# Attention: the queries' rotary product on VectorE instead of GpSimd

## The chip, the cores and the metric

The kernel runs on one core of a Trainium2 chip. That core has a matrix engine (TensorE, PE in the profile; PEld is its weight load), three engines for elementwise work (VectorE = DVE, ScalarE = ACT, GpSimd = POOL), a queue engine that issues most transfers (SyncE = SP), and 16 DMA engines. The engines run their own instruction queues in order and wait for each other through semaphores. The metric is the device time of one execution in microseconds.

## The reference

The program is two layers of a diffusion backbone for 512 latent tokens and 256 context tokens, width 1024, in float32. Layer 0 mixes tokens by windowed grouped-query attention (16 query heads of 64, 4 key heads), layer 1 by a chunked retention. Each layer ends in a gated feed-forward block. Only the latent stream is returned. The change lies in layer 0, in the step between the query projection and the scores:

```python
q_x, k_x, v_x = jnp.split(h_x @ w_qkv, [qd, qd + kvd], axis=-1)
q_x = rope_2d(rms_norm(q_x.reshape(B, S, N_HEADS, HEAD_DIM), q_gain), tables)

def rotate_axis(x, cos, sin):
    x1, x2 = jnp.split(x, 2, axis=-1)
    return jnp.concatenate([x1 * cos - x2 * sin, x1 * sin + x2 * cos], axis=-1)
```

So each query element is multiplied by a cosine, its partner 16 places away by a sine, and the two products are added. Context queries (`s == 1` in the kernel) have no positions and skip the step. After it come scores over a window of 128 and all context keys, a softmax with a sink logit, the value product and the output projection.

## The kernel before

Activations lie transposed, with channels on the 128 partitions and tokens along the free dimension. A query tile `j` (0 to 7) holds two heads: 128 channels by 512 latent and 256 context tokens. Every large product is made of three reduced-precision matmuls (`mm3`, lines 148 to 150): weight and activation are each split into a high and a low part. The splits of weights (`next_w`, lines 140 and 141) and of other operands (`split`, lines 165 and 166) cost one ScalarE copy and one VectorE subtraction each.

`make_q(j)` returns four pieces: projections of the latent and context tokens, with `shape(s)` behind each, and `norms()`. `shape(0)` is what changes. ScalarE takes the projection out of PSUM into `qn` (564) and its squares into `sq` (565). VectorE writes the partner channels into `sw` by a shuffle (569). GpSimd multiplies `qn` by the cosines (570) while VectorE multiplies `sw` by the sines (571), and VectorE adds the two (572). ScalarE and VectorE then split the result into high and low parts per head (578 to 581). `norms()` computes the inverse root mean squares by a small matmul (590) and short instructions (593, 597); they enter the softmax as scales. The keys' step, `rope_key`, has the same four elementwise instructions all on VectorE.

An attention block is one key head with its four query heads and 128 queries, 24 blocks in all: four head groups, each with four latent and two context blocks. For each head, `score` copies the bound for the row maximum (668, GpSimd), multiplies queries by keys (684, TensorE), and adds the mask and takes the row minimum (685, VectorE). For each pair of heads there follow a small product (691, VectorE), two exponentials with row sums (101, ScalarE), a reciprocal (695, VectorE) and two normalisations in SBUF (698, GpSimd). `turn` transposes the probabilities by the identity (707, TensorE) and copies them out of PSUM (709, ScalarE and VectorE alternately). `output` multiplies by the values (719) and copies the result (734, VectorE). After the first three groups `split_o` splits their results for the output projection (165, 166).

The program gives the order of the pieces: the tiles 0 and 1 first, then two further tiles within each of the first three head groups, after their second and fourth blocks. In that part only the first tile's TensorE work is in an order written out by hand. Everywhere else a planner takes each engine's instructions, gives each a cost of its own and orders the queue by it, so blocks, projections and splits are interleaved. The order is fixed when the kernel is built. A projection's matmuls thus lie between the scores, transposes and value products of other blocks, and the first output-projection tiles (lines 148 to 150 on the `h` tiles) between those of the last group. SP's queue brings the weights (line 122), then the residual streams (174, 179).

Of the kernel before, what the change touches and what calls it, by code (L numbers as in the profile page):

```python
# [49 lines left out]
def dit_kernel(ctx, tc, xT, cT, crow, small, consts, masks, tabs0, tabs1, jtab, adaQ, adaN, adaT, wst, out):  # L50
    nc = tc.nc
    mult, add, sub = ALU.mult, ALU.add, ALU.subtract
# [9 lines left out]
    def T(pool, cols, tag, bufs, dt=F32):  # L62
        return pool.tile([P, cols], dt, tag=tag, bufs=bufs, name=tag)

    def pj(n=512):
        return T(psJ, 512, "pj", 2)[:, :n]
# [69 lines left out]
    def next_w(pool, own=2, raw=None):  # L136

        raw = raw or w_raw()
        hi, lo = w_parts(pool, own)
        nc.scalar.copy(hi, raw)  # L140
        nc.vector.tensor_tensor(lo, raw, hi, op=sub)  # L141
        return hi, lo

    def mm3(o, w, x, first, last):

        whi, wlo = w
        xhi, xlo = x
        nc.tensor.matmul(o, whi, xhi, start=first, stop=False)  # L148
        nc.tensor.matmul(o, wlo, xhi, start=False, stop=False)  # L149
        return nc.tensor.matmul(o, whi, xlo, start=False, stop=last)  # L150
# [32 lines left out]
    def t_sq(n):  # L183
        return T(rp, 512, "sq", 2)[:, :n]

    def t_hn(n):
        return T(rp, 512, "hn", 2)[:, :n]

    def t_y(s):
        return T(rp, NTOK[s], f"y{s}", 1)  # L190

    def neg_half_rstd(y, z, tot, count):

        lnexp(y, tot, AF.Ln, scale=1.0 / count, bias=eps)
        lnexp(y, y, AF.Exp, scale=-0.5)
        nc.scalar.activation(z, y, AF.Square, scale=0.5 / math.sqrt(count))
        nc.vector.scalar_tensor_tensor(z, tot, count * EPS, z, add, mult)
        nc.vector.scalar_tensor_tensor(y, z, -0.75, y, add, mult)
# [194 lines left out]
    rope0 = T(akv, 1024, "rope0", 1)  # L393
# [153 lines left out]
    def make_q(j, raw=None):  # L547

        w = next_w(ap, 1, raw)
        qs = T(ap, 64, "qs", 4)[:, 0:36].rearrange("p (f n) -> p f n", f=3)
        sqs, o = [], [None, None]

        def part(s, k0, k1):
            if k0 == 0:
                o[s] = pj(NTOK[s])
            for k in range(k0, k1):
                mm3(o[s], (w[0][:, k * P:(k + 1) * P], w[1][:, k * P:(k + 1) * P]), h[s][k], k == 0, k == KT - 1)

        def shape(s):
            n = NTOK[s]
            sq, qn = t_sq(n), t_hn(n)
            nc.scalar.activation(qn, o[s], AF.Identity, scale=qk_gain[:, 0:1])
            nc.scalar.activation(sq, o[s], AF.Square)
            sqs.append(sq)
            if s == 0:
                sw = t_y(s)
                nc.vector.stream_shuffle(sw, qn, swap16)
                nc.gpsimd.tensor_tensor(qn, qn, rope0[:, 0:512], op=mult)  # L570
                nc.vector.tensor_tensor(sw, sw, rope0[:, 512:1024], op=mult)
                nc.vector.tensor_tensor(qn, qn, sw, op=add)
            qa = T(ap, 512, "q", 9, F32R)
            if s == 0:
                qb = T(ap, 512, "q", 9, F32R)
            else:
                qa, qb = qa[:, 0:SC], qa[:, SC:2 * SC]
            nc.scalar.copy(qa[0:64, :], qn[0:64, :])
            nc.scalar.copy(qb[64:128, :], qn[64:128, :])
            nc.vector.tensor_tensor(qa[64:128, :], qn[0:64, :], qa[0:64, :], op=sub)  # L580
            nc.vector.tensor_tensor(qb[0:64, :], qn[64:128, :], qb[64:128, :], op=sub)
            q[2 * j, s] = qa
            q[2 * j + 1, s] = qb

        def norms():
            tot = pj(12)
            for s, sq in enumerate(sqs):
                for b in range(NTOK[s] // P):
                    c = 8 * s + 2 * b
                    nc.tensor.matmul(tot[:, c:c + 2], sq[:, b * P:(b + 1) * P], bd[:, 0:P:64], start=True, stop=True)  # L590
            y, u, z = qs[:, 0], qs[:, 1], qs[:, 2]
            neg_half_rstd(y, z, tot, HD)
            nc.vector.scalar_tensor_tensor(u, tot, HD * EPS, y, add, mult)
            ue = u.rearrange("p (b e) -> p e b", e=2)
            for e in range(2):
                hd = 2 * j + e
                nc.vector.tensor_scalar(ue[:, e], ue[:, e], nsink[:, hd:hd + 1], -4.0 / HD, op0=mult, op1=mult)
                stats[hd] = qs

        def first():  # L600
            part(0, 0, 5)

        def second():
            part(0, 5, KT)
            shape(0)
            part(1, 0, 3)

        def third():
            part(1, 3, KT)
            shape(1)  # L610

        return [first, second, third, norms]
# [1178 lines left out]
```

## Time and profile before

| | |
|---|---|
| runs (3) | 1774.48 to 1779.74 us, median 1777.0 us |
| profiled execution | 1777.24 us, span 1775.5 us |
| TensorE busy | 1717.1 us (97%) |
| VectorE busy | 1356.0 us (76%) |
| ScalarE busy | 841.2 us (47%) |
| GpSimd busy | 134.4 us (8%) |
| mean granted TensorE clock | 0.994 |
| line 570 on GpSimd | 8 instructions, 12.9 us, first start 88.9 us, last 254.4 us |

Times in the traces are microseconds from the start of the span. Attention runs from about 88 us to 328 us; before it lie the modulation and the key and value projections, after it the output projection, the feed-forward block and layer 1. Matmuls are pipelined, so their recorded durations overlap: the spacing of their starts says what one costs. A number in square brackets behind an instruction is the time its engine stood idle just before it, with the instruction that ended the wait. A wait for several instructions is put down to the one that came last.

### The profile page before, as it was taken

How to read it: one execution, taken by the hardware profiler on the slowest of the kernel's cores; microseconds unless marked ns; L12 is line 12 of the kernel's file. 1: busy time of each engine (PE TensorE's matmuls, PEld its weight loads, DVE VectorE, ACT ScalarE, POOL GpSimd, SP SyncE). 2: the span in 40 equal slices, each digit the busy share in tenths (PEclk: the TensorE clock that was granted, in tenths of full speed). 3: DMA queues.
4: the chain of work that ended last, by engine and by line, in shares of the span. 5: the costliest groups of instructions: out<-in, count | busy, mean ns of one | idle time of the engine just before them, and what ended most of it. 6: DMA issues, size and time to landing. Idle time of an engine off the chain costs nothing.

```text
span 1775.5 us, 27602 instructions
## 1 busy us (share of the span) xinstructions
PE 1717.1 (97%) x10852; PEld 1527.1 (86%) x10852; DVE 1356.0 (76%) x2365; ACT 841.2 (47%) x1477; POOL 134.4 (8%) x275
## 2 busy tenths in 40 slices
PE   6899999999999999999998999999999999999999
PEld 4777776789999999999978788898897899999998
DVE  6697786788778778777789758758758798777774
ACT  5477676456333434242465534524524564445432
POOL 0035344100000000000010000000000000000000
PEclk9999999999999999999999999999999999999999
DMA  8610002434243534343342534434433323333222
GB/s 334 239 36 25 25 1 84 145 107 165 73 154 107 157 116 143 119 146 111 123 133 88 164 106 132 153 102 132 153 104 119 95 72 116 94 112 107 92 88 83
DMA packets 59891, 206.68 MB, mean 116 GB/s; under 512 B 6641, under 2 KB 7025, under 8 KB 59505
## 3 DMA queue, kind: packets, MB, share of 16 engines
q1 hardware_dynamic: 52848, 179.75, 31.2%
q0 software_dynamic: 6912, 25.17, 4.8%
q8 instruction: 85, 1.39, 0.3%
q14 instruction: 46, 0.37, 0.1%
HBM read 202.80 MB, written 2.10 MB: 115 GB/s over the span
## 4 chain that ended last, share of the span: by engine, by line
PE 74%; DVE 13%; ACT 4%; DMA 4%; issue 2%; POOL 2%; SPq 0%; ACTq 0%; DVEq 0%; POOLq 0%
PE Y L835 13%; PE Z L835 6%; PE pj L148 6%; PE pj L150 6%; PE pj L149 6%; PE Y L1180 4%; PE Z L1193 3%; PE X L835 3%; DVE wlo L166 3%; DMA wraw<-in_wst_dram 2%; PE pT L707 2%; PE S L684 2%; PE pO L719 2%; PE pj L1193 2%; PE X L1180 1%
## 5 line engine op out<-in xcount | busy, mean ns | idle before, releaser
L165 ACT CAST whi<-wraw 128x1024 fp32r<-128x1024 f32 x177 | 185.5, 1051 | 305.3 <-PE Z L150 71.5
L166 DVE TENSOR_TENSOR wlo<-wraw,whi 128x1024 fp32r<-128x1024 f32 x177 | 215.7, 1221 | 42.1 <-ACT whi L165 41.6
L835 PE MATMUL Y<-aq,whi 128*128 128x384 f32 x640 | 173.7, 335 | 0.9 <-ACT hn L973 0.8
L253 DVE SCALAR_TENSOR_TENSOR res<-pj,mod,res 128x512 f32<-128x512 f32 (+1 forms) x112 | 81.6, 729 | 70.3 <-PE pj L150 69.1
L141 DVE TENSOR_TENSOR wlo<-wraw,whi 128x1024 fp32r<-128x1024 f32 x80 | 97.9, 1223 | 36.6 <-ACT whi L140 36.0
L140 ACT CAST whi<-wraw 128x1024 fp32r<-128x1024 f32 x80 | 84.0, 1050 | 75.9 <-DMA wraw<-in_wst_dram 26.8
L835 PEld LDWEIGHTS Y<-aq,whi 128*128 128x128 f32 x640 | 116.6, 188 | 2.4 <-ACT hn L973 2.0
L271 DVE CUSTOM_DVE_ANT_0 y<-adaw,crow,small_sb 128x1024 bf16<-128x1024 f32 x64 | 81.9, 1279 | 33.7 <-DMA adaw<-in_adaT_dram 33.5
L835 PE MATMUL Y<-aq,wlo 128*128 128x384 f32 x320 | 107.0, 334 | 0.0
L101 ACT ACTIVATE pr<-pr,stat,qs 128x513 f32<-128x513 f32 (+2 forms) x96 | 74.2, 775 | 30.7 <-DVE stat L691 29.8
L1193 PE MATMUL Z<-whi,sA 128*128 128x512 f32 x256 | 81.0, 392 | 0.6 <-ACT whi L165 0.6
L698 POOL TENSOR_SCALAR pr<-pr,stat 128x512 f32<-128x512 f32 (+2 forms) x96 | 68.0, 721 | 86.7 <-DVE stat L695 66.6
L148 PE MATMUL pj<-ax,whi 128*128 128x512 f32 x176 | 68.7, 390 | 1.0 <-DVE res L253 1.0
L150 PE MATMUL pj<-ax,whi 128*128 128x512 f32 x176 | 68.6, 390 | 0.0
L149 PE MATMUL pj<-ax,wlo 128*128 128x512 f32 x176 | 68.5, 389 | 0.0
L707 PE MATMUL pT<-const_sb,pr 128*128 128x128 f32 x352 | 58.0, 284 | 10.9 <-POOL pr L698 8.6
L148 PE MATMUL pj<-act,whi 128*128 128x512 f32 x168 | 66.0, 393 | 0.1
L149 PE MATMUL pj<-act,wlo 128*128 128x512 f32 x168 | 65.9, 392 | 0.0
L707 PEld LDWEIGHTS pT<-const_sb,pr 128*128 128x128 f32 x352 | 38.8, 140 | 31.3 <-POOL pr L698 19.2
L150 PE MATMUL pj<-act,whi 128*128 128x512 f32 x168 | 65.5, 390 | 0.0
L268 POOL DMA_DIRECT2D adaw<-in_adaT_dram x48 | 25.6, 533 | 520.6 <-DVE mod L271 420.8
L685 DVE CUSTOM_DVE_ANT_0 pr<-S,mask,qs 128x256 f32<-128x256 f32 (+1 forms) x96 | 53.1, 567 | 14.3 <-PE S L684 7.9
(518 smaller groups left out, 5273.7 us busy)
## 6 DMA issues: line engine op xcount, KB each, us to landing
wraw<-in_wst_dram SPq DMA_DIRECT2D x238, 512.0 KB, 3.6
adaw<-in_adaT_dram POOLq DMA_DIRECT2D x48, 512.0 KB, 3.9
wx<-in_wst_dram SPq DMA_DIRECT2D x24, 512.0 KB, 4.6
adan<-in_adaQ_dram SPq DMA_DIRECT2D x16, 512.0 KB, 8.0
adan<-in_adaN_dram SPq DMA_DIRECT2D x16, 512.0 KB, 8.5
res<-in_xT_dram SPq DMA_DIRECT2D x16, 256.0 KB, 5.5
adaw<-in_adaT_dram SPq DMA_DIRECT2D x8, 512.0 KB, 4.0
aq<-in_adaN_dram SPq DMA_DIRECT2D x12, 256.0 KB, 6.4
```

Of the source, the lines that this page charges most:

```text
L140: nc.scalar.copy(hi, raw)
L141: nc.vector.tensor_tensor(lo, raw, hi, op=sub)
L148: nc.tensor.matmul(o, whi, xhi, start=first, stop=False)
L149: nc.tensor.matmul(o, wlo, xhi, start=False, stop=False)
L150: return nc.tensor.matmul(o, whi, xlo, start=False, stop=last)
L165: nc.scalar.copy(hi, t)
L166: return nc.vector.tensor_tensor(lo, t, hi, op=sub)
L271: after(nc.vector.tensor_tensor_reduce(junk, w, cr[:, s * 1024:(s + 1) * 1024], 1.0, sm_t[:, C_ADAB + l * 48 + j:C_ADAB + l * 48 + j + 1], ...
L707: nc.tensor.transpose(tp[:, a * P:(a + 1) * P], self.pr[(0, 2, 1, 3)[a]][:, ki * P:(ki + 1) * P], ident)
L835: nc.tensor.matmul(o, p, r, start=first and k + i == 0, stop=k == 3 and i == 2, skip_group_check=not first)
L1180: ins = nc.tensor.matmul(o[:, e * SC:(e + 1) * SC], p[:, ws], r, start=first and k + e + i == 0, stop=k == 3 and i == 2, skip_group_check= ...
L1193: ins = nc.tensor.matmul(o, p, r, start=first and k + i == 0, stop=k == 3 and i == 2, skip_group_check=not first)
```

## The change

The product of the queries with the cosines is issued on VectorE's queue instead of GpSimd's, for each of the eight latent query tiles. Operands, result and the instructions around it are the same. The planner orders the queues anew with it.

```diff
             if s == 0:
                 sw = t_y(s)
                 nc.vector.stream_shuffle(sw, qn, swap16)
-                nc.gpsimd.tensor_tensor(qn, qn, rope0[:, 0:512], op=mult)
+                nc.vector.tensor_tensor(qn, qn, rope0[:, 0:512], op=mult)
                 nc.vector.tensor_tensor(sw, sw, rope0[:, 512:1024], op=mult)
                 nc.vector.tensor_tensor(qn, qn, sw, op=add)
```

## The prediction

> **What bounds the kernel now.** I read the page's busy shares first, then the attention stage by windows, then who waits for whom inside it, then single places on the timeline.
>
> ```profile
> PE 1717.1 (97%) x10852; PEld 1527.1 (86%) x10852; DVE 1356.0 (76%) x2365; ACT 841.2 (47%) x1477; POOL 134.4 (8%) x275
> ```
>
> TensorE is busy for 97% of the span and GpSimd (POOL) for 8%. The line that changes (570) runs only inside the attention stage, so that stage is looked at alone. The columns of the next view are the stretch, then busy time and instructions of PE, PEld, VectorE (DVE), ScalarE (ACT) and POOL, then the granted TensorE clock, the DMA share and GB/s.
>
> ```profile
> 88.00:328.00 240.00, 225.06 (x1541) 175.44 (x1540) 186.69 (x569) 163.22 (x383) 95.36 (x200) 1.00 0.13 42
> 325.00:330.00 5.00, 3.38 (x10) 2.11 (x7) 2.85 (x4) 4.65 (x7) 0.00 (x0) 0.65 0.94 335
> 330.00:335.00 5.00, 5.00 (x16) 3.97 (x15) 1.29 (x2) 2.24 (x3) 0.00 (x0) 0.66 0.42 163
> ```
>
> In the 240 us of attention TensorE stands idle for 15 us, VectorE is busy 78% and GpSimd 40%. So TensorE's own work still sets most of the stage, and all that any edit of the other engines can win here is those 15 us plus what hides inside matmuls that start late. The last two rows show the stage's end: the granted clock falls to 0.65 and 0.66, which is (0.35 + 0.34) x 5 = 3.45 us of full speed lost.
>
> ```profile
> PEld pT L707 <- POOL pr L698: 19.2, 40, 1.5
> DVE hn L572 <- POOL hn L570: 3.2, 3, 1.2
> ```
>
> The first wait (in 95 to 328 us) is TensorE's largest in the stage: the transposes of the probabilities (707) wait 19.2 us in 40 places for the normalisation on GpSimd (698). The second (88 to 328 us) is what VectorE loses to the line that changes: its add (572) waits 3.2 us in 3 places for GpSimd's product (570).
>
> **The change, part by part.** One instruction of each of 8 query projections leaves GpSimd's queue and enters VectorE's. Nothing is added or removed; no DMA moves with it.
>
> ```profile
> L570 POOL TENSOR_TENSOR hn<-hn,rope x8: 1274/1780/1800, 88.9 to 254.4; 128x512 f32<-128x512 f32 x8
> L571 DVE TENSOR_TENSOR y<-y,rope 128x512 f32<-128x512 f32 x8 | 6.6, 822 | 0.1
> L572 DVE TENSOR_TENSOR hn<-hn,y 128x512 f32<-128x512 f32 x8 | 5.8, 731 | 3.3 <-POOL hn L570 3.2
> L581 DVE TENSOR_TENSOR q<-hn,q 64x512 fp32r<-64x512 f32 x8 | 7.4, 930 | 0.2
> ```
>
> GpSimd gives up 8 products of 1.27 to 1.80 us. VectorE's own product of the same shape (571) is the nearest row for the new one; its mean of 822 ns includes one blocked case of 1.77 us, seen below, without which it is (6.6 - 1.77) / 7 = 0.69 us. I take 0.69 us a product, 8 x 0.69 = 5.5 us; the upper bound is 8 x 1.77 = 14.2 us. VectorE at the same time drops the 3.2 us in which it stood before line 572, and the 1.77 - 0.69 = 1.1 us of the blocked case. Its load grows by about 1.2 us net out of 240, so it does not become the bound by its sum. What counts is three places where VectorE's queue held a reciprocal (695) behind the add that waited for GpSimd, while GpSimd's next normalisation, and TensorE behind it, waited for that reciprocal. The first, query tile 4:
>
> ```profile
> 173.28 1.79 POOL L570 TENSOR_TENSOR hn<-hn,rope 128x512 f32<-128x512 f32 x1
> 173.23 0.69 DVE L571 TENSOR_TENSOR y<-y,rope 128x512 f32<-128x512 f32 x1
> 173.84 0.42 DVE L734 COPY res<-pO 128x256 f32<-128x256 f32 x1
> 175.11 0.69 DVE L572 TENSOR_TENSOR hn<-hn,y 128x512 f32<-128x512 f32 x1 [0.85 <-POOL hn L570]
> 175.72 0.15 DVE L695 RECIPROCAL stat<-stat 128x2 f32<-128x2 f32 x1
> 175.97 2.00 POOL L698 TENSOR_SCALAR pr<-pr,stat 128x640 f32<-128x640 f32 x2 [0.90 <-DVE stat L695]
> 176.83 0.42 PEld L707 LDWEIGHTS pT<-const_sb,pr 128*128 128x128 f32 x4 [1.38 <-POOL pr L698]
> 178.03 0.20 PEld L707 LDWEIGHTS pT<-const_sb,pr 128*128 128x128 f32 x2 [0.63 <-POOL pr L698]
> ```
>
> A VectorE product takes 173.84 - 173.23 = 0.61 us of the queue from start to start. With both products there, the add starts at 173.23 + 2 x 0.61 + 0.42 = 174.87 instead of 175.11: 0.24 us earlier, because most of GpSimd's 1.79 us already lay beside VectorE's own work. The built order of the changed kernel keeps the neighbours here. Query tiles 6 and 7:
>
> ```profile
> 230.24 0.68 DVE L571 TENSOR_TENSOR y<-y,rope 128x512 f32<-128x512 f32 x1
> 232.11 0.69 DVE L572 TENSOR_TENSOR hn<-hn,y 128x512 f32<-128x512 f32 x1 [1.19 <-POOL hn L570]
> 233.05 0.15 DVE L695 RECIPROCAL stat<-stat 128x2 f32<-128x2 f32 x1
> 234.16 0.42 PEld L707 LDWEIGHTS pT<-const_sb,pr 128*128 128x128 f32 x4 [0.81 <-POOL pr L698]
> 235.36 0.20 PEld L707 LDWEIGHTS pT<-const_sb,pr 128*128 128x128 f32 x2 [0.62 <-POOL pr L698]
> ...
> 254.57 1.77 DVE L571 TENSOR_TENSOR y<-y,rope 128x512 f32<-128x512 f32 x1
> 256.27 0.41 DVE L166 TENSOR_TENSOR hc<-res,hc 128x256 fp32r<-128x256 f32 x1
> 256.60 0.68 DVE L572 TENSOR_TENSOR hn<-hn,y 128x512 f32<-128x512 f32 x1
> 257.87 0.15 DVE L695 RECIPROCAL stat<-stat 128x2 f32<-128x2 f32 x1
> 258.96 0.31 PEld L707 LDWEIGHTS pT<-const_sb,pr 128*128 128x128 f32 x3 [1.33 <-POOL pr L698]
> 260.05 0.31 PEld L707 LDWEIGHTS pT<-const_sb,pr 128*128 128x128 f32 x3 [0.79 <-POOL pr L698]
> ```
>
> For tile 6 the new order puts the copy of 734 (0.42) ahead of the add: the add ends at 230.24 + 1.22 + 0.42 + 0.61 = 232.49, and the reciprocal starts there instead of at 233.05: 0.56 us earlier. For tile 7 the two products end at 254.57 + 1.22 = 255.79, the split of 166 (0.33 from start to start) follows, and the add starts at 256.12 instead of 256.60: 0.48 us earlier. Together -1.3 us on TensorE's path. Tile 5's reciprocal waited for its exponential anyway, so the product put ahead of it costs nothing:
>
> ```profile
> 201.70 0.17 DVE L695 RECIPROCAL stat<-stat 128x2 f32<-128x2 f32 x1 [1.08 <-ACT pr L101]
> ```
>
> Tiles 0 to 3 have no wait of this kind; there the new product is either hidden in VectorE's idle time or costs 0.61 us each, so 0 to +2.4 us; I take +0.3, nearest to the row of tile 5, where it is hidden.
>
> [...]
>
> **The new order.** The planner that orders each engine's queue sees another duration, so the built order of the changed kernel differs on all engines from the first query tiles to near the end of attention, and nowhere after it. In-order TensorE waits where too little other work stands between a head pair's scores (684) and its first transpose (707). I counted that work in both orders by these spacings: 0.22 us for a 512-wide matmul, 0.12 for a 256-wide one, 0.87 / 8 for a transpose, 2.35 / 20 for a value product.
>
> ```profile
> 139.62 0.39 PE L150 MATMUL pj<-h,whi 128*128 128x512 f32 x1
> 139.84 0.28 PE L148 MATMUL pj<-hc,whi 128*128 128x256 f32 x1
> 139.96 0.28 PE L149 MATMUL pj<-hc,wlo 128*128 128x256 f32 x1
> ...
> 142.46 0.87 PE pT L707 x8
> 144.94 2.35 PE pO L719 x20
> ```
>
> What that work has to cover is the softmax of a pair:
>
> ```profile
> L685 DVE CUSTOM_DVE_ANT_0 pr<-S,mask,stat 128x384 f32<-128x384 f32 x32 | 19.2, 606 | 0.7 <-PE S L684 0.2
> L101 ACT ACTIVATE pr<-pr,stat,qs 128x641 f32<-128x641 f32 x32 | 29.4, 920 | 21.7 <-DVE stat L691 21.6
> L101 ACT ACTIVATION_READ_ACCUMULATOR pr<-pr,stat,qs 128x1 f32 x96 | 18.0, 188 | 0.0
> L698 POOL TENSOR_SCALAR pr<-pr,stat 128x640 f32<-128x640 f32 x32 | 26.9, 853 | 40.4 <-DVE stat L695 26.3 <-DVE stat L691 14.1
> ```
>
> That is 0.61 + 2 x (0.92 + 0.19) + 2 x 0.85 = 4.5 us, to which two small VectorE steps and the queues come; I take 6 us, with 7 as the other end. Over the 41 pairs whose order was counted, what is missing against 6 us grows by 5.5 us where the new order is tighter and falls by 5.5 where it is looser; against 7 us it is 10.7 and 9.6. So the new order costs 0 to +1.1 us; I take 0. The signs stand in different places: looser mostly in the first two head groups, tighter in early blocks of the last (7.6 to 5.2 us and 7.4 to 5.8 for two pairs). One load of an output-projection weight moves behind the twelve residual loads on SP's queue; it is cast only after the last attention block, long after those have been issued, so I count it at nothing; if the residual loads were held up until then, the first output projections would wait for them and for it.
>
> **The sum** stands against the profiled execution's 1777.24 us (span 1775.5 and 1.7 around it), which is 0.2 above the median of the runs, 1777.0. -1.3 + 0.3 + 0 = -1.0, so 1776.2 us: no change that a measurement of this kernel can tell, since about 0.3% (5.3 us) is needed for that.
>
> **Rivals.**
> - *Faster: the normalisation waits go.* If the three reciprocals come early enough that TensorE no longer waits there at all, 1.38 + 0.63 + 0.81 + 0.62 + 1.33 + 0.79 = 5.6 us go: 1771.7. If with that the half-clock stretch at the end of attention also falls away, 3.45 more: 1768.2. For it speaks that line 698 is TensorE's largest wait; against it that most of the 1.79 us lay beside other work.
> - *Slower: the new order.* If the tighter places cost TensorE in full and the looser ones give nothing back, since another engine then holds them, it is 5.5 to 10.7 us more: 1781.7 to 1786.9. It decides once the unreturned part passes 6.3 us. For it speaks that the tighter blocks lie late, in the last head group, where nothing follows to catch up; against it that the totals are equal.
> [...]
>
> **How the numbers follow.** The forecast, no telling change around 1776.2, gets 0.48; its own range is 1772 to 1782. The faster rival gets 0.24, the order 0.20 and the blocked products 0.08. So faster 0.24, same 0.48, slower 0.28. The range reaches from the faster rival's lower end, 1768, to the slower rivals' upper one, 1787, with a tenth left out on each side for a second half-clock stretch more or less.
>
> **What would show it.** In the changed profile the product of 570 is on VectorE at 0.69 us, or up to 1.77 beside 698; VectorE's wait for GpSimd at 572 is gone; the waits of 707 for 698 near query tiles 4, 6 and 7 are shorter by 0.2 to 0.6 us, not gone; and the stage's end, the first matmul after the 0.65 clock, stands within 5 us of where it is now. I am wrong if 707's total wait for 698 moves by more than 5 us either way, if the waits grow in the last head group (from 265 us on), or if the number of half-clock stretches changes.

## The result

The changed kernel takes 1770.9 us (median of 14 runs, 1768.61 to 1774.81) against 1777.08 us (14 runs of the kernel before beside them, 1774.48 to 1779.74). The ratio is 0.9966, 95% interval [0.9958, 0.9974]: 6.1 us faster, a little over what a measurement of this kernel can tell. The prediction had 1776.2, so the time lies below the forecast's own range of 1772 to 1782 and inside the whole range of 1768 to 1787.

The profiled execution took 1770.2 us, span 1768.4, 7.1 less than the one before. The page of the changed kernel, its busy shares:

```profile
PE 1717.1 (97%) x10852; PEld 1528.9 (86%) x10852; DVE 1359.0 (77%) x2373; ACT 840.9 (48%) x1477; POOL 119.7 (7%) x267
```

TensorE is busy for the same 1717.1 us. Its waits in attention (95 to 328 us), and the groups of the rotary step (88 to 328 us), in the changed kernel:

```profile
PEld pT L707 <- POOL pr L698: 15.2, 38, 1.3
...
L570 DVE TENSOR_TENSOR hn<-hn,rope 128x512 f32<-128x512 f32 x8 | 5.5, 689 | 0.1
L572 DVE TENSOR_TENSOR hn<-hn,y 128x512 f32<-128x512 f32 x8 | 5.5, 684 | 0.1
L571 DVE TENSOR_TENSOR y<-y,rope 128x512 f32<-128x512 f32 x8 | 5.5, 684 | 0.0
```

The eight products are on VectorE at 0.69 us (0.680 to 0.693), the add (572) no longer waits, and 707 waits 4 us less for the normalisation. Where the gain ends is seen at the first output projection, the first matmul on the `h` tiles that waits for its weight's copy (140). Before:

```profile
326.59 0.29 PEld L148 LDWEIGHTS pj<-h,whi 128*128 128x128 f32 x1 [1.75 <-ACT whi L140]
```

After:

```profile
319.48 0.29 PEld L148 LDWEIGHTS pj<-h,whi 128*128 128x128 f32 x1 [1.75 <-ACT whi L140]
```

It starts 7.11 us earlier, behind the same wait of 1.75 us. That is the whole difference of the spans (7.1): nothing was won or lost later. 0.6 of it was there when attention began (the first shuffle, 569, starts at 88.05 and 87.44), where the two programs are the same. So the measure in what follows is the **stage**: from the first shuffle to the first output projection. By windows (length, then busy time of PE, PEld, VectorE, ScalarE and GpSimd, then granted clock), before and after:

```profile
88.05:326.59 238.54, 223.92 (x1539) 174.80 (x1537) 185.23 (x567) 161.83 (x381) 95.36 (x200) 1.00 0.12 40
```

```profile
87.44:319.48 232.04, 222.73 (x1539) 174.16 (x1537) 187.04 (x575) 161.27 (x381) 80.60 (x192) 1.00 0.13 41
```

TensorE's idle time falls from 14.6 to 9.3 us. Some executions have half-clock stretches (the granted clock is 0.50 there) inside the stage; what they cost (length times one minus the granted clock, summed over windows of about 1 us) is taken off, and the stage at full clock is then 238.5 us before and 231.9 after, 6.6 less.

The place of query tile 4 in the changed kernel, on VectorE, GpSimd and TensorE:

```profile
174.17 0.68 DVE L572 TENSOR_TENSOR hn<-hn,y 128x512 f32<-128x512 f32 x1
174.77 0.16 DVE L695 RECIPROCAL stat<-stat 128x2 f32<-128x2 f32 x1
...
175.02 2.01 POOL L698 TENSOR_SCALAR pr<-pr,stat 128x640 f32<-128x640 f32 x2 [3.76 <-DVE stat L695]
...
175.54 0.28 PE L150 MATMUL pj<-hc,whi 128*128 128x256 f32 x1
175.66 0.95 PE L590 MATMUL pj<-const_sb,sq 128*128 128x2 f32 x8
176.46 0.48 PE L684 MATMUL S<-kc,q 128*128 128x256 f32 x2
176.78 0.82 PE L707 MATMUL pT<-const_sb,pr 128*128 128x128 f32 x6
```

The waits of 1.38 and 0.63 us are gone. The normalisation still takes 2.0 us and starts 0.95 us earlier, of which 0.61 us is the earlier start of the stage; but ahead of the transposes now stand the rest of the tile's projection, its norms (590) and two score matmuls (684), which came behind them before. So two things changed at once, the engine of the product and the order of all queues.

### The profile page after: what moved, and what is told of

Read it like the earlier page. It is cut to its first block, busy times and chain, and to the rows that moved or that the text cites. A ratio compares the mean times of both kernels' runs of the same rounds, so it can differ in the third digit from the quotient of the medians.

```text
span 1768.4 us, 27618 instructions
## 1 busy us (share of the span) xinstructions
PE 1717.1 (97%) x10852; PEld 1528.9 (86%) x10852; DVE 1359.0 (77%) x2373; ACT 840.9 (48%) x1477; POOL 119.7 (7%) x267
## 4 chain that ended last, share of the span: by engine, by line
PE 76%; DVE 13%; DMA 4%; ACT 3%; issue 2%; POOL 1%; SPq 0%; ACTq 0%; DVEq 0%; POOLq 0%
PE Y L835 14%; PE Z L835 7%; PE pj L149 6%; PE pj L148 6%; PE pj L150 6%; PE Z L1193 4%; PE X L835 3%; DMA wraw<-in_wst_dram 3%; DVE wlo L166 2%; PE pT L707 2%; PE Y L1180 2%; PE pj L1193 2%; PE pO L719 2%; PE S L684 2%; PE X L1180 1%
## 5 line engine op out<-in xcount | busy, mean ns | idle before, releaser
L707 PEld LDWEIGHTS pT<-const_sb,pr 128*128 128x128 f32 x352 | 39.1, 140 | 27.8 <-POOL pr L698 15.2
L685 DVE CUSTOM_DVE_ANT_0 pr<-S,mask,qs 128x256 f32<-128x256 f32 (+1 forms) x96 | 53.0, 568 | 12.5 <-PE pT L707 6.1
L835 PE MATMUL Y<-sA,whi 128*128 128x256 f32 x304 | 60.8, 283 | 0.1
```

What stands on the lines that cost most here:

```text
L707: nc.tensor.transpose(tp[:, a * P:(a + 1) * P], self.pr[(0, 2, 1, 3)[a]][:, ki * P:(ki + 1) * P], ident)
L835: nc.tensor.matmul(o, p, r, start=first and k + i == 0, stop=k == 3 and i == 2, skip_group_check=not first)
```

## The experiments

Two theories. **Engine**: the gain is the move itself, a shorter chain in each query tile and a freer GpSimd. **Order**: the gain is the new order that the planner makes for every engine. The two can be parted, since the instructions of both builds are the same but for the engine of eight of them: a list of instruction numbers for each engine, tied as issue order without any wait, holds the queues in either order.

The stage figures below come from one profiled execution each. How well they repeat can be seen where two runs have the same program and order. Counted from the stage's start, e4 stands within 0.02 us of the kernel before at each of the six block copies (734) ahead of its first moved place, and e7 within 0.2 us of the changed kernel up to 204 us. So the lists by themselves cost nothing that shows, and a stage figure is good to about 0.2 us, but for one meeting of two engines near 272 us, told under the single places.

### The move and the order apart

Run e1, product on VectorE, old order:

```diff
-                nc.gpsimd.tensor_tensor(qn, qn, rope0[:, 0:512], op=mult)
+                nc.vector.tensor_tensor(qn, qn, rope0[:, 0:512], op=mult)
...
+    keep_order(tc, order)   # each engine's queue in the order of the kernel before
```

> The cosine product is on VectorE, directly ahead of the sine product (571), and every queue is held in the order of the kernel before. Engine theory (the gain comes from the move itself: GpSimd's 1.8 us leaves the chain of the query tile and GpSimd's queue): 1769 to 1773 us, 4 to 8 below the kernel before; 707's wait for 698 falls from 19.2 to about 15 us and the first output projection comes 5 to 7 us earlier. Order theory (the gain comes from the order that the planner makes of the moved step): 1775 to 1778, within 2 us of the kernel before; 707 still waits 18 to 19 us. The prediction's own sum for the three places is -1.3 + 0.3: 1776.

Run e2, product on GpSimd, new order:

```diff
+    keep_order(tc, order)   # each engine's queue in the order of the changed kernel
```

> The cosine product stays on GpSimd, and every queue is held in the order of the changed kernel (on GpSimd the product stands where the planner puts it among the others). Engine theory: 1776 to 1779, no gain. Order theory: 1769 to 1773, the whole gain or nearly so, though the add (572) goes on waiting 3 us or more for the product. If both count, the gains of this run and of the run with the old order add up to the 6 us of the change.

Measured: e1 0.9985 [0.9975, 0.9996], median 1776.1 us; e2 0.9965 [0.9953, 0.9978], median 1772.0 us. The stage of e1, by windows:

```profile
88.28:325.45 237.17, 224.32 (x1538) 174.78 (x1536) 187.89 (x575) 161.64 (x381) 80.31 (x192) 1.00 0.12 40
```

and of e2:

```profile
87.12:321.01 233.89, 223.39 (x1538) 174.37 (x1537) 185.19 (x567) 161.29 (x381) 94.37 (x200) 1.00 0.13 41
```

The order alone wins 4.6 us of the stage with the product still on GpSimd; the move alone wins 1.3. 707 waits 17.3 us for 698 in e1 and 16.9 in e2 (95 to 328 us), between the 19.2 before and the 15.2 after the change. The order theory stands. In whole times e2 (0.9965) and the change (0.9966) cannot be told apart; it is the stage that parts them, by 2.0 us. The prediction's sum for the move was -1.0; how much of the 1.3 is chance is told under the single places. e1 also shows its single places, by the waits of TensorE in the old order:

```profile
176.87 0.42 PEld L707 LDWEIGHTS pT<-const_sb,pr 128*128 128x128 f32 x4 [1.04 <-POOL pr L698]
...
203.36 0.42 PEld L707 LDWEIGHTS pT<-const_sb,pr 128*128 128x128 f32 x4 [1.00 <-POOL pr L698]
...
234.24 0.42 PEld L707 LDWEIGHTS pT<-const_sb,pr 128*128 128x128 f32 x4 [0.19 <-POOL pr L698]
...
258.67 0.31 PEld L707 LDWEIGHTS pT<-const_sb,pr 128*128 128x128 f32 x3 [0.85 <-POOL pr L698]
```

Tile 4: 1.38 to 1.04, so 0.34 (forecast 0.24). Tile 6: 0.81 to 0.19, so 0.62 (0.56). Tile 7: 1.33 to 0.85, so 0.48 (0.48). At tile 5, counted at nothing, the wait grows from 0.40 (202.71 us in the kernel before) to 1.00.

### What the product costs at all

Runs e3 (old order) and e12 (new order) cut the product to one column:

```diff
-                nc.gpsimd.tensor_tensor(qn, qn, rope0[:, 0:512], op=mult)
+                nc.gpsimd.tensor_tensor(qn[:, 0:1], qn[:, 0:1], rope0[:, 0:1], op=mult)
...
+    keep_order(tc, order)   # e3: order of the kernel before; e12: of the changed kernel
```

> The cosine product is cut to one column and stays on GpSimd, with every queue in the order of the kernel before (all but one column of the query is left without its cosine). It takes GpSimd's 1.3 to 1.8 us away without giving VectorE anything. Engine theory: 4 to 8 us faster, 1769 to 1773, at least as much as with the product on VectorE. Order theory: within 2 us of the kernel before, 1775 to 1778. The prediction's places would then each gain their 0.7 to 1.2 us of waiting at 572 instead of 0.2 to 0.6: about -3, 1774.

> The cosine product cut to one column on GpSimd (all but one column of the query is left without its cosine), every queue in the order of the changed kernel. With the product in full the stage took 233.9 us at full clock on GpSimd and 231.9 on VectorE in this order; in the old order one column won 3.0 us over the product on VectorE. If VectorE's queue costs the same in the new order: 229 us. If the new order covers it: 231 to 232 us, and the change has all that can be had from this product.

Measured: e3 0.9972 [0.9960, 0.9985], stage 234.2 us; e12 0.9955 [0.9939, 0.9971], stage 231.5 us. The stage at full clock in a square:

| product | old order | new order |
|---|---|---|
| on GpSimd | 238.5 (before) | 233.9 (e2) |
| on VectorE | 237.2 (e1) | 231.9 (after) |
| one column | 234.2 (e3) | 231.5 (e12) |

In the old order the eight products on VectorE cost 237.2 - 234.2 = 3.0 us of the stage; in the new order 231.9 - 231.5 = 0.4. The order theory had e3 within 2 us of before; it fell there, since without the product the old order is 4.3 us faster. The engine theory had at least as much as on VectorE, 1769 to 1773, and the prediction's places about 1774; the median was 1773.7. So order and product are not two separate gains: the new order covers most of what this product costs (cover is other work that TensorE has in its queue while a chain runs on the other engines), and better on VectorE (0.4 left) than on GpSimd (2.4). But that is not all it does: with the product cut to one column it still wins 234.2 - 231.5 = 2.7 us. About half of its gain is therefore no cover of this product, and no run here says what it is.

### Where in the stage

Runs e6 and e7 have the product on VectorE and change from the new order to the old one at a point of the stage:

```diff
+    keep_order(tc, order)   # order of the changed kernel up to 165.6 us (e6) or 204 us (e7), then of the kernel before; SP's queue as before throughout
```

> Cosine product on VectorE; every queue in the order of the changed kernel up to 165.6 us of its trace (before tile 4), after that in the order of the kernel before. Counted by TensorE's idle time, the order wins 0.55 us and a start 0.4 us earlier up to there, and 4.5 us behind: first output projection at 324.5 (325.45 with the old order throughout, 319.48 with the new one). If instead the early head groups carry the order's gain: 319.5 to 321.

> As the run before, with the change of order at 204 us, behind query tiles 4 and 5. By TensorE's idle time (1.67 against 3.52 us up to there, and the earlier start): first output projection at 323.0, so half of the order's gain is made by then and half at tiles 6 and 7. By the block copies, which run 4.9 us ahead at this place: 320.5, nearly the whole gain.

Measured: e6 0.9982 [0.9969, 0.9996], stage 236.6; e7 0.9973 [0.9962, 0.9984], stage 233.4. Against e1's 237.2 the new order wins 0.6 us up to 165.6, 3.1 between there and 204 us (query tiles 4 and 5), and 233.4 - 231.9 = 1.5 behind. The starts themselves (325.99 and 321.63 us) also hold a different start of the stage (87.70 and 88.20) and, in e6, 1.7 us of half clock. The idle count had half of the order's gain made by 204 us; measured were 3.7 of 5.3.

### The single places

Run e4 is the kernel before, product on GpSimd, its own order, but for one place on TensorE:

```diff
 TensorE's queue, by lines, behind the value products and fifteen projection matmuls
-707 x4, 148, 707 x2, 149, 150, 148, 149, 150, 707 x8, 148, 149, 707 x4, 150, 590 x4, 684 x4
+148, 149, 150, 148, 149, 150, 148, 149, 150, 590 x4, 684 x2, 707 x6, 707 x8, 707 x4, 684 x2
```

> The kernel before, the cosine product on GpSimd and all queues in its own order, but for one place on TensorE: the last nine projection matmuls of query tile 4, its norms (590, first half) and two of its score matmuls (684) stand ahead of the six transposes (707) that waited 1.38 and 0.63 us, as they do in the order of the changed kernel. Place theory (what the new order wins is cover at the few transposes that wait for the query tile's own rotary step): those two waits fall below 0.3 us, TensorE's idle time before the first output projection falls from 14.6 to about 13 us, and that projection starts at 325.0 instead of 326.59 (1.6 earlier, 1.0 to 2.4). Rival (the waits only move to the next place, so that one place alone wins nothing and the gain needs the whole order): it starts within 0.4 us of 326.59.

Run e5 adds two such places:

```diff
 tile 6
-590 x4, 707 x4, 684, 707 x2, 684
+590 x4, 684 x2, 707 x4, 707 x2
 tile 7
-707 x6, 150, 148, 149, 150, 148, 149, 707 x8, 150, 590 x4
+150, 148, 149, 150, 148, 149, 150, 707 x6, 707 x8, 590 x4
```

> As the run with one place, and two more places on TensorE: at tile 6 two score matmuls (684) stand ahead of the transposes that waited 0.81, and at tile 7 the last seven projection matmuls stand ahead of the transposes that waited 1.33 us. Place theory: 1.6 + 0.2 + 0.8, so the first output projection starts at about 324.0, 2.6 earlier (1.8 to 4.0), and the time is 1774 to 1775, still with every cosine product on GpSimd. Rival (one place cannot be had without the others): less than 1 us earlier, time 1776 to 1778.

Measured: e4 0.9987 [0.9974, 1.0001], stage 236.7 us; e5 0.9985 [0.9973, 0.9997], stage 236.1 us. The first output projections start at 326.81 and 327.58 us, which by the letter of the expectations speaks for the rival; but these starts are of no use, since the stage began at 88.45 and 86.32 us and lost 1.7 and 5.1 us to half clock. At full clock the stage is 1.9 and 2.4 us shorter, near the 1.6 and 2.6 expected, but not for the reason given. TensorE in e4, at tile 4 and later:

```profile
176.99 0.95 PE L590 MATMUL pj<-const_sb,sq 128*128 128x2 f32 x8
177.80 0.49 PE L684 MATMUL S<-kc,q 128*128 128x256 f32 x2
178.12 0.82 PE L707 MATMUL pT<-const_sb,pr 128*128 128x128 f32 x6
```

The two waits are gone, but the stage is only 0.1 us ahead at the next block copy (734) and 0.7 at the one after it. 1.1 of the 1.9 us fall at quite another place, near 272 us, where nothing was edited. There the kernel before has, on GpSimd, VectorE and TensorE:

```profile
269.73 2.50 POOL L698 TENSOR_SCALAR pr<-pr,stat 128x256 f32<-128x256 f32 x2 [0.57 <-DVE stat L691]
269.88 0.95 DVE L166 TENSOR_TENSOR h<-res,h 128x256 fp32r<-128x256 f32 x2
270.75 1.21 DVE L141 TENSOR_TENSOR wlo<-wraw,whi 128x1024 fp32r<-128x1024 f32 x1
...
272.28 0.42 PEld L707 LDWEIGHTS pT<-const_sb,pr 128*128 128x128 f32 x4 [1.47 <-POOL pr L698]
```

and e1, with the same instructions in the same order at this place:

```profile
269.56 1.37 POOL L698 TENSOR_SCALAR pr<-pr,stat 128x256 f32<-128x256 f32 x2 [0.57 <-DVE stat L691]
269.70 0.96 DVE L166 TENSOR_TENSOR h<-res,h 128x256 fp32r<-128x256 f32 x2
270.59 1.41 DVE L141 TENSOR_TENSOR wlo<-wraw,whi 128x1024 fp32r<-128x1024 f32 x1
...
270.98 0.42 PEld L707 LDWEIGHTS pT<-const_sb,pr 128*128 128x128 f32 x4 [0.45 <-POOL pr L698]
```

In the kernel before the second normalisation ended only behind the weight's split (141; 272.23 against 271.96 us), and the two normalisations took 2.50 instead of 1.37 us; in e1, e3, e4 and e5, which have the old order here, they took 1.37, and TensorE's wait behind them is 0.45 us in e1 instead of 1.47. What decides is not shown: by the recorded starts the second normalisation is ahead of the split both times, by 0.2 us in the kernel before (270.54 and 270.75) and by 0.55 in e1 (270.04 and 270.59). Some 1.1 us of the gain of each of these runs in the old order is this one meeting; without it e1 wins 0.2, e4 0.8, e5 1.3 and e3 3.2 us, of the 4.6 us between before and e2 3.5 are left, and of the change's 6.6 us 5.5. Moving cover by hand thus gave about half of what it was to give, and the three places together 1.3 of the 3.5 us that the order wins with the product on GpSimd; where the rest comes from stays open.

Run e11 does it on the changed kernel, at the five places with the longest waits left:

```diff
 TensorE's queue, by lines (the transposes that waited, and what now stands ahead of them)
+684 x4 ahead of 707 x6 (156 us); 150, 148, 149, 150 ahead of the second 707 x3 (200 us);
+684, 590 x2 ahead of 707 x2 (231 us); 149, 150, 148, 149 ahead of 707 x6 (254 us);
+149, 150, 148 ahead of the second 707 x3 (278 us)
```

> The changed kernel with five places of its order on TensorE moved by hand: score or projection matmuls that stand just behind the transposes (707) with the longest waits left (1.06 near 156 us, 0.79 near 200, 0.57 near 231, 0.53 near 254 and 1.32 near 278 us) stand ahead of them. Place theory (cover at the places where a transpose waits is what counts): the waits fall by 0.9 + 0.45 + 0.35 + 0.45 + 0.7 = 2.9 us, so the stage takes 229 us at full clock (231.9 in the changed kernel) and the time is about 1768. Rival (what is taken from behind a wait is missing at the next one): 231 to 233 us, and 1770 to 1772.

Measured: 0.9961 [0.9946, 0.9975], which is not told apart from the changed kernel's 0.9966; stage 231.1 us, 0.7 less than the changed kernel. The waits did fall:

```profile
PEld pT L707 <- POOL pr L698: 12.5, 38, 0.8
```

from 15.2 to 12.5 us, nearly the 2.9 expected, and the stage kept 0.7 of it. By the stage the rival stands: most of what is taken from behind one wait is missing later. Its median of 1768.2 us over five runs is the lowest of the kernels that compute all, and the one that the place theory named; but the intervals do not part it from the change.

### Is a new order always a gain

Runs e8 and e9 move the product for half of the tiles and leave the order to the planner:

```diff
-                nc.gpsimd.tensor_tensor(qn, qn, rope0[:, 0:512], op=mult)
+                (nc.vector if j > 3 else nc.gpsimd).tensor_tensor(qn, qn, rope0[:, 0:512], op=mult)   # e8; e9: j < 4
```

> The cosine product on VectorE for query tiles 4 to 7 alone, every queue as the planner orders it for this kernel. The measure is the attention stage from the first shuffle (569) to the first output projection at full clock: 238.5 us before, 231.9 after the change. Systematic theory (the planner makes a better order where it knows the query tile's chain to be shorter): the gain lies at the tiles that were moved, 3.1 of it at tiles 4 and 5 and 1.5 behind them, so 233 to 234.5 us, and 1772 to 1773 in all. Lottery theory (any new order lands some us away on either side, whatever was moved): no tie to the tiles; anything from 233 to 241.

> The cosine product on VectorE for query tiles 0 to 3 alone, every queue as the planner orders it for this kernel. Systematic theory: the order of the changed kernel wins only 0.6 us before tile 4, so 237 to 238.5 us for the stage and 1775.5 to 1777.5 in all. Lottery theory: anything from 233 to 241, and the order of the later tiles, where nothing was moved, changes as well.

Run e10 moves the sine product to GpSimd instead, beside the cosine:

```diff
-                nc.vector.tensor_tensor(sw, sw, rope0[:, 512:1024], op=mult)
+                nc.gpsimd.tensor_tensor(sw, sw, rope0[:, 512:1024], op=mult)
```

> The opposite edit: the sine product (571) goes to GpSimd too, so that both products of a query tile are there, one behind the other, and VectorE only adds; every queue as the planner orders it for this kernel. Systematic theory: the query tile's chain grows by 1.8 - 0.7 = 1.1 us or more at every tile, and the planner can cover only part of it: the stage takes 239.5 to 245 us, 1778 to 1784 in all. Lottery theory: anything from 235 to 243, faster than before included. If VectorE's queue is what costs (the run with one column was 3.0 us better than the product on VectorE in the same order), the stage could gain instead, since VectorE loses eight products of 0.61 us: 236 to 238.

Measured: e8 0.9974 [0.9965, 0.9984], stage 234.9; e9 1.0008 [0.9995, 1.0022], stage 239.0; e10 1.0069 [1.0052, 1.0085], stage 243.1. e8 and e10 follow what was moved: tiles 4 to 7 carry most of the gain, and a longer chain costs. e9 does not: with four products moved its stage is 0.5 us longer, where the systematic theory had it up to 1.5 shorter. And the two halves do not add up to the whole: -3.7 and +0.5 against -6.6. In e9 the stage ran 0.7 us ahead near 166 us and lost that and 0.5 more at the later tiles, where the product stayed on GpSimd and only the order was new. TensorE's waits there:

```profile
201.13 0.31 PEld L707 LDWEIGHTS pT<-const_sb,pr 128*128 128x128 f32 x3 [1.41 <-POOL pr L698]
...
215.00 0.42 PEld L707 LDWEIGHTS pT<-const_sb,pr 128*128 128x128 f32 x4 [1.22 <-POOL pr L698]
...
234.00 0.42 PEld L707 LDWEIGHTS pT<-const_sb,pr 128*128 128x128 f32 x4 [1.56 <-POOL pr L698]
```

So both theories of that comparison hold in part: the planner makes use of a shorter chain, and beside it the order moves by a few us with nothing in its favour. In e10 VectorE lost eight products and stood waiting instead:

```profile
L572 DVE TENSOR_TENSOR hn<-hn,y 128x512 f32<-128x512 f32 x8 | 6.0, 751 | 12.2 <-POOL y L571 12.2
```

and in its profiled execution 6.8 us of half clock inside the stage came on top of the 4.6 us at full clock, which makes the stage 11.4 us longer. The expected time, 1778 to 1784, left that out; the median is 1787.1. Each of the three half-clock stretches (near 106, 181 and 270 us) begins behind a wait of TensorE (it was busy for 0.69 of the 2.04 us before 105.11, for 0.94 of the 3.07 us before 180.95 and for 0.72 of the 2.09 us before 269.22), but that the waits bring them is not shown: in the kernel before TensorE is busy for 1.73 of the 3.41 us from 257.00 on, and no such stretch follows.

## Why the prediction was right and wrong

- **The forecast**, no telling change around 1776.2, was missed on the fast side: 1770.9 is below its own range. The whole range held only because the faster rival had drawn it down to 1768, and, as told below, that rival was near by its number and not by its means.
- **The bound** was right: TensorE's idle time in the stage, 14.6 us, and what hides inside matmuls that start late. 5.3 of the 6.6 us came out of the idle time. For the rest, TensorE's recorded busy time fell by 223.9 - 222.7 = 1.2 us with the same 1539 matmuls; through which of them is open.
- **The product's price** was right: 8 x 0.69 = 5.5 us, each of the eight between 0.680 and 0.693 us. VectorE's busy time in the stage grew by 187.0 - 185.2 = 1.8 us. That this is near the forecast 1.2 is chance: the 1.2 took off 3.2 us in which VectorE stood idle, which is no load. The load alone was forecast to grow by 5.5 - 1.1 = 4.4 us, and other instructions of VectorE got 2.6 us shorter beyond that. The blocked products, given 0.08, did not come. That a VectorE product takes 1.77 us beside line 698 was the author's estimate, and no run shows it: the one product of that length, 571 at 254.57 us before, ran beside 570 on GpSimd (254.37, 1.42 us), and the longest of the lines 570 to 572 on VectorE beside 698, before and after, is the add at 122.56 us before, 1.00 us.
- **The three places** were right within 0.1 us each: 0.34, 0.62 and 0.48 against 0.24, 0.56 and 0.48 (e1). At tile 7 the add had not waited for GpSimd, as the prediction says of all three; there it was the sine product, 1.77 us long, that held VectorE's queue. Tile 5, counted at nothing because its reciprocal waited for the exponential, cost 0.6: that wait was no cover. In e1 the product stands ahead of the small product (691) for which the pair's exponentials wait, and 691 starts at 200.36 instead of 199.71 us, so the exponentials and the reciprocal come later too. Tiles 0 to 3 were put at +0.3; where tile 4 begins, e1's stage stood 0.2 later than that of the kernel before.
- **The sum of the move**, -1.0, was near by luck: e1's stage is 1.3 us shorter, of which 1.1 is the meeting near 272 us. 0.2 us is left, too little to be told from nothing.
- **"The new order costs 0 to +1.1 us; I take 0"** is the step that failed. It won 4.6 us with the product on GpSimd (3.5 without the meeting near 272 us) and 5.3 with it on VectorE. I had summed what cover is missing over 41 pairs against one softmax of 6 or 7 us, and tighter and looser places balanced. But the softmax is not of one length: where a query tile's rotary step stands in VectorE's queue between a pair's exponentials and its reciprocal, the chain is longer than elsewhere (the waits of 1.38 and 1.33 us are there), and a sum over all pairs hides that cover is worth more at such a place. That is the part of the explanation that the runs bear out, with about half of the expected worth in e4 and e5; why the order wins 2.7 us even without the product is open. The prediction saw at tile 4 that VectorE's neighbours stayed the same and did not look at TensorE's queue there, where nine more projection matmuls, the norms and two scores had been put ahead of the transposes. The signs were also wrong for the last head group. By windows from the block copy at 257.54 to the one at 279.18 us, before, and from 252.16 to 273.06, after:

```profile
257.54:279.18 21.64, 18.71 (x135) 14.36 (x134) 18.43 (x61) 14.34 (x39) 9.32 (x23) 1.00 0.28 93
```

```profile
252.16:273.06 20.90, 20.00 (x144) 15.42 (x143) 18.64 (x66) 15.19 (x41) 8.12 (x23) 1.00 0.19 53
```

TensorE's idle time between them fell from 2.9 to 0.9 us; it had been forecast to grow there. About 1.1 us of the 2.0 is the meeting near 272 us; between e1 (257.25 to 278.00 us), where the meeting went the other way, and the changed kernel it falls from 1.5 to 0.9.

- **The faster rival** was nearest, 1771.7 against 1770.9, and at its places: of its 5.6 us of waits 1.38 + 0.63 went wholly, 0.81 and 1.33 shrank to 0.57 or less, and 0.79 stayed at 0.68. But its means, reciprocals that come early enough, gave 1.4 us (e1: 0.34 + 0.62 + 0.48); the rest came with the order, and longer waits stand at other places instead (1.06 us near 156, 1.32 near 278). That its number is so near is therefore luck. It had been given 0.24.
- **The half-clock stretch** behind the stage stayed. By windows of the changed kernel:

```profile
319.00:324.00 5.00, 4.20 (x9) 3.02 (x10) 3.62 (x4) 4.95 (x7) 0.00 (x0) 0.52 0.90 301
324.00:329.00 5.00, 5.00 (x19) 3.98 (x19) 0.36 (x3) 1.15 (x1) 0.00 (x0) 0.80 0.29 99
```

(0.48 + 0.20) x 5 = 3.4 us of full speed lost, as before (3.45).

- **The signs of being wrong** were too coarse: 707's wait moved by 4.0 us, inside the 5 that were named, while the stage moved by 6.6. Two of the marks that were to show the forecast right did fail: the waits at tile 4 are gone, and the stage's end moved by 7.1 us, not within 5. TensorE's idle time up to the first output projection would have told. The moved weight load cannot be told apart from the rest; TensorE waits the same 1.75 us for that weight's copy in both.

## What to carry to other kernels

Where a planner orders the queues, moving one instruction is two changes, and the order can be the larger one: hold the old order with the new engine, and the new order with the old engine, before crediting either. To judge an order, do not weigh its total cover against a mean chain; take the few places where the chain is longest and read, on the engine that bounds, what stands ahead of the instruction that waits. That names the places, not the gain: cover put there by hand gave a quarter (e11) to a half (e4, e5) of what its waits promised. And compare stages from a common start at full clock, since starts in single profiles here differed by over 2 us with the same program before them.

## What had not been expected of the hardware

**Half-clock stretches come in pieces of one size.** In the profiles there are stretches, in the stage or just behind it, in which the granted clock is 0.50 and which cost 1.7 or 3.4 us of full speed. One lies behind the stage of the kernel before, the changed kernel, e3 and e11 (3.4 us each) and of e1, e4, e5, e7 to e10 and e12 (about 1.7 us each); others lie inside it, as one near 236 us in e4, where the kernel before has the same order and no such stretch (granted clock 1.00 in its stage). In e4:

```profile
232.90:236.30 3.40, 2.32 (x16) 2.03 (x17) 3.00 (x6) 2.75 (x7) 2.00 (x2) 0.91 0.00 0
...
234.00:239.00 5.00, 4.57 (x24) 4.19 (x25) 3.66 (x8) 2.82 (x9) 1.03 (x1) 0.67 0.00 0
```

(0.33 x 5 = 1.7 us), and in e11:

```profile
252.00:262.00 10.00, 9.11 (x58) 7.75 (x56) 7.97 (x21) 6.48 (x16) 2.84 (x6) 0.78 0.21 73
```

(0.22 x 10 = 2.2 of the 3.4 us there). One piece more or less is 0.1 to 0.2% of the time, up to a little over half of what the change itself brings: e11's profiled execution took 1774.2 us, the longest of its five runs. TensorE did not stand still when the stretch in e4 began: it was busy for 2.32 of the 3.4 us in which the clock begins to fall. At a clock of 0.50 the two costs are stretches of 1.7 / 0.5 = 3.4 and 3.4 / 0.5 = 6.8 us; by windows of 1 us the one behind the stage of the kernel before reaches from about 326.5 to 333.4 us. What begins a stretch and what sets its length, no run here shows.

**One meeting of VectorE and GpSimd goes either way in the same order, and is worth 1.1 us** of the stage (269.7 us in the kernel before, 2.50 against 1.37 us in e1). The lengths run against each other: the second normalisation takes 1.69 us in the kernel before and 0.89 in e1, the split 1.21 and 1.41. What lengthens the one or the other is not shown; the normalisation's recorded start is the earlier one in both.
